# Decoder trunk on one core: modulation rows summed in 256 KB blocks from two buffers of their own, and four reorderings of issue

## The chip, the cores and the metric

The kernel runs on one core of a Trainium2 chip. Its time is the device time of one execution in microseconds; the median of several runs is what is compared. Engines are named as in the profile: PE (TensorE, the matrix engine) with PEld (its weight loads), DVE (VectorE), ACT (ScalarE), POOL (GpSimd) and SP (SyncE, which here does little else than issue DMAs). Each engine works through its own queue in order; a semaphore makes an instruction wait for another engine's or a DMA's result, and everything behind it on the same queue waits too.

## What is computed

One layer of a conditioned decoder trunk, sequence 512, width 1024, cut to its lines of substance:

```python
mod = silu(c) @ w_ada + b_ada                                   # (1024) @ (1024, 6*1024)
shift1, scale1, gate1, shift2, scale2, gate2 = split(mod, 6)
h = rmsnorm(x, norm1_g) * (1 + scale1) + shift1
qa, ka, va, qd, kd, vd, ga, gd = split(h @ w_in)                # input projection
out_a = sliding_window_attention(qa, ka, va, sinks)             # 8 heads, 2 kv heads, window 128
out_d = diff_attention(qd, kd, vd, lam, subln_g)                # 4 heads, softmax1 - lam * softmax2
merged = sigmoid(ga) * (out_a @ w_branch_swa) + sigmoid(gd) * (out_d @ w_branch_diff)
x = x + gate1 * (merged @ w_out)
h2 = rmsnorm(x, norm2_g) * (1 + scale2) + shift2
a, g = split(h2 @ w_up)                                         # 2 x 2816
a = causal_conv3(a) + conv_b
x = x + gate2 * ((gelu(a) * g) @ w_down)
return rmsnorm(x, final_g)
```

The modulation vector `mod` has six parts. The first two are needed at once; the other four (gate1, shift2, scale2, gate2, columns 2D to 6D of `w_ada`) are needed only behind the attention. Those four are the "modulation rows" here.

## The kernel before, in words

Everything stays in float32 accuracy: a float32 operand is split into a high part (cast on ACT) and a low part (subtraction on DVE), and each product takes three matmuls. So each weight tile of 512 KB passes through a raw buffer, gets an ACT cast `..._h` (L115) and a DVE subtraction `..._l` (L116), and then feeds PE. There are four raw buffers (`raw_tile`, tag "raw").

The kernel goes through these stages: the first modulation parts and the first norm (up to about 60 us); the attention with the input projection in between (to about 300 us); the branch gates and the merge; the output projection (`oc`, `wo`), the second norm and its transposes (`th`, about 345 to 375 us); the up products (`up`, from about 372 us on) and the down products (`dc`).

In the attention stage PE's order is written out by hand (`manual_schedule` for the tensor engine): scores, transposes and values of a window pair or of a differential block stand at fixed places, and between them `fill(n)` issues n steps of whatever projection is next (`units`: q, k and v of the differential heads, gates, branch products). Each step counts one tick. ACT's and DVE's order in this stage is not written by hand: a planner places their instructions, by priority and by when it holds their inputs for ready. SP's DMA order follows from the same planning. `tc.high_priority(offset=...)` lifts an instruction's priority. Behind the output projection the order of DVE, ACT, PE and POOL is written out by hand as well.

In the names of the trace: `sw`, `st`, `mx`, `nm`, `lsum` belong to the softmax of the window heads (four pairs; `tp` are its transposes on PE, `oa` and `outal` its values), `sd`, `dmx`, `dls` to the softmax of the differential heads (four heads of four blocks; `td` are its transposes on PE). `qkv` are the evictions of a head's projections.

The modulation rows are no matmul: `ada_rows` is a generator that `fill` advances every `ADA_EVERY` ticks. Each step loads two 128-row blocks of one half part (`ra`, 128x2x512, 512 KB, from SP), and adds both on DVE into `arow`, weighted by the column `cs` of silu(c): the first of eight blocks by a multiplication (L776), the other seven by multiply and add (L778). There are 4 parts x 2 halves x 8 blocks = 64 sums. When a half is done, `ada_spread` adds over the partitions by four small matmuls (`pr`), copies `row` on ACT (L794) and writes it to DRAM from POOL, from where it is later read as broadcast rows (`g1b`, `g2b`) or columns. Behind tick 20 a sum has a raised priority.

Further on the change touches: `add_head` (evictions of q and k), `diff_values` (`of`, and `rstd_m2`, a root that is worked out by DVE, POOL and DVE), the loads of the up weights of block 1 (`wa1_0`, `wa1_1`, cast by ACT and DVE as `early`, L1287 and L1291), and the modulation of the transposed rows (`mod_one`: `braw`<-`th`, L1255 on ACT, L1253 on DVE).

Of the kernel before, what the change touches and what calls it, by code (L numbers as in the profile page):

```python
# [8 lines left out]
F32 = mybir.dt.float32  # L9
# [5 lines left out]
P = 128  # L15
# [12 lines left out]
HP = 100000  # L28
ST = 6
ADA_LAG = 1  # L30
ADA_EVERY = 8
ADA_EASY = 20
ADA_START = 4
V_LAG = 13
# [19 lines left out]
def kernel(  # L54
# [130 lines left out]
    def rstd_m2(dst, ssq, n, d, wpool, plus=None):  # L185
        rstd_end(dst, *rstd_start(ssq, n, d, wpool, plus), n, wpool)
# [239 lines left out]
    def evac(hi, lo, src, scale=None):  # L426
        if scale is None:
            nc.scalar.copy(hi, src)
            nc.vector.tensor_sub(lo, src, hi.bitcast(F32))
        else:  # L430
            nc.scalar.activation(hi, src, AF.Copy, scale=scale)
            nc.vector.scalar_tensor_tensor(lo, src, scale, hi.bitcast(F32), ALU.mult, ALU.subtract)
# [184 lines left out]
    def add_head(h):  # L617
        def q(wts):
            t = heads[h] = ap.tile([P, 6, S], F32R, tag="qkv", bufs=2, name=f"qkv{h}")
            o = fbank(f"pq{h}")  # L620
            yield from steps(o, wts, hT, KT)
            evac(t[:, 0], t[:, 1], o, 2.0 ** (2 * h - 1))

        def k(wts):
            t = heads[h]
            o = fbank(f"pk{h}")
            yield from steps(o, wts, hT, KT)
            evac(t[:, 2], t[:, 3], o)

        def v(wts):  # L630
            t = heads[h]
            o = fbank(f"pw{h}")
            yield from steps(o, wts, hT, KT)
            vT = ap.tile([P, S], F32, tag="tmp", bufs=2, name=f"vT{h}")
            with tc.high_priority(offset=HP):
                nc.scalar.copy(vT, o)

            def turn():
                pv = tbank(f"pv{h}")
                for m in range(NT):  # L640
                    nc.tensor.transpose(pv[:, m * P : (m + 1) * P], vT[:, m * P : (m + 1) * P], ident)
                evac(t[:, 4], t[:, 5], pv)

            after(V_LAG, turn)

        for run, col in ((q, COL_QD), (k, COL_KD), (v, COL_VD)):
            units.append((lambda col=col: load_cols(win, col + h * P, f"w{col}_{h}"), run))
# [73 lines left out]
    def diff_values(h):  # L721
        t, (aTh, aTl) = heads[h], aTs[h]
        o = vbank(f"od{h}")
        for k in range(NT):
            q0 = k * P
            mm3(
                o[:, q0:], t[:, 4, k * P : (k + 1) * P], t[:, 5, k * P : (k + 1) * P],
                aTh[:, k * AW + q0 : k * AW + 512], aTl[:, k * AW + q0 : k * AW + 512],
                k == 0, k == NT - 1,
            )  # L730
        sq = ap.tile([P, S], F32, tag="tmp", bufs=2, name=f"sq{h}")
        of = ap.tile([P, S], F32, tag="of", bufs=2, name=f"of{h}")
        nc.scalar.activation(sq, o, AF.Square)
        nc.scalar.activation(of, o, AF.Copy, scale=sublnc)

        def stats():
            pss = tbank(f"pss{h}", (P, NT))
            for n in range(NT):
                nc.tensor.matmul(pss[:, n : n + 1], sq[:, n * P : (n + 1) * P], ones[:, 0:1], start=True, stop=True)
            rs = ap.tile([P, NT], F32, tag="drs", bufs=2, name=f"drs{h}")  # L740
            rstd_m2(rs, pss, NT, P, ap)

            def spread():
                rb = tbank(f"rb{h}")
                for n in range(NT):
                    nc.tensor.transpose(rb[:, n * P : (n + 1) * P], rs[:, n : n + 1].to_broadcast([P, P]), ident)
                nc.vector.tensor_mul(of, of, rb)
                split(outd[0][:, h], outd[1][:, h], of)

            after(NORM_LAG, spread)  # L750

        after(STAT_LAG, stats)


    mod_rows = tc.dram_tile([4, D], F32, name="mod_rows")

    def ada_load(idx, hf, k):
        c0 = (2 + idx) * D + hf * S
        r = raw_tile([P, 2, S], f"ra{idx}{hf}_{k}")
        nc.sync.dma_start(r, wada[k * P : (k + 2) * P, c0 : c0 + S].rearrange("(a p) n -> p a n", p=P))  # L760
        return r


    def ada_rows():
        todo = [(idx, hf, k) for idx in range(4) for hf in range(2) for k in range(0, KT, 2)]
        r = ada_load(*todo[0])
        yield
        for (idx, hf, k), job in zip(todo, todo[1:] + [None]):
            nxt = ada_load(*job) if job else None
            if k == 0:  # L770
                ac = big.tile([P, S], F32, tag=("sq2", "g2b1")[hf], name=f"arow{idx}{hf}")
            with tc.high_priority(offset=HP // 2) if tick[0] > ADA_EASY else ExitStack():
                for a in range(2):
                    cc = cs[:, k + a : k + a + 1]
                    if k + a == 0:
                        nc.vector.tensor_scalar_mul(ac, r[:, a], cc)  # L776
                    else:
                        nc.vector.scalar_tensor_tensor(ac, r[:, a], cc, ac, ALU.mult, ALU.add)  # L778
            if k == KT - 2:
                after(ADA_LAG, lambda idx=idx, hf=hf, ac=ac: ada_spread(idx, hf, ac))  # L780
            r = nxt
            yield


    def ada_spread(idx, hf, ac):
        pr = tbank(f"pr{idx}{hf}", (P, P))
        for g in range(4):
            gs = slice(32 * g, 32 * g + 32)
            nc.tensor.matmul(
                pr[gs], ones[:, gs], ac[:, g * P : (g + 1) * P], start=True, stop=True, tile_position=(0, 32 * g)  # L790
            )
        row = big.tile([P, P], F32, tag="g2b0", name=f"row{idx}{hf}")
        with tc.high_priority(offset=HP):
            nc.scalar.copy(row, pr)  # L794
        nc.gpsimd.dma_start(  # L795
            mod_rows[idx, hf * S : (hf + 1) * S].rearrange("(g n) -> g n", g=4), row[0:P:32]
        )
# [88 lines left out]
        add_gate_a(j)  # L886
    fill(4)
    diff_values(DIFF_HEADS - 1)
    while units or loaded or current:
        fill(1)  # L890
    at.close()


    bp = pool("mlp")

    def gpart(i, shape, name, dt=F32):
        return bp.tile(shape, dt, tag=f"gT{i}", name=name)
# [122 lines left out]
    bl = big.tile([P, 3, 4, 256], F32R, tag="hlA", name="bl")  # L1020
    braw = {}
    oacc = eight("oc")
    wo = [load_rows(wout, k, f"wo{k}", g1b) for k in range(KT)]

    def add_and_stat(acc, dst, x, wpool, name):
# [27 lines left out]
    early_w = [  # L1053
        big.tile([P, 2, 4, 256], F32R, tag=g, name=f"early{i}") for i, g in enumerate(("kvA", "kvB", "outh", "outl"))
    ]
    W, R = {}, {}

    def load_raw(dst, blocks):
        nc.sync.dma_start(dst, upblock(*blocks[0]))
# [44 lines left out]

    load_a(0, 0)
    load_a(0, 1)
    load_a(1, 0)
    load_a(1, 1)
    st = gpart(3, [P, 2, 4, 256], "s1_t1")
    t1n = st[:, 1]  # L1110
    R[0, "s1"] = load_raw(st[:, 0], [(0, 1, 0), (0, 1, 1)])
# [257 lines left out]
    mul_slot(0, "p2", (0,))  # L1369
    for g in (0, 1):  # L1370
        for kk in range(2):
            mod_one(b12[:, ks(g)], tps[g], g, kk)
        if g == 0:
            cast_w(0, "m5")
    for g in (2, 3):
        tps[g] = turn2(2, g)
    mul_slot(0, "p2", (1,))
    mul_slot(1, "p1", (1,))
    mul_slot(1, "p2")
    bV += [tbank("up6"), tbank("up7")]  # L1380
    V.tensor_sub(t1n[:, q0], b11[:, q0], b12[:, q0])
    low_w(0, "m5")
    V.tensor_sub(t1n[:, q1], b11[:, q1], b12[:, q1])
    sum_w(0, "m6")
    hi_t(0, t1n, q0)
    for kk in range(2):
# [429 lines left out]
```

## Time and profile before

| | |
|---|---|
| median of 3 runs | 702.29 us (701.95 to 703.43) |
| the profiled execution | 705.5 us, of which the span from first to last instruction is 703.6 us |
| mean granted TensorE clock | 0.992 |
| PE busy | 683.6 us, 97% of the span |
| DVE busy | 572.0 us, 81% |
| ACT busy | 375.8 us, 53% |
| POOL busy | 82.5 us, 12% |
| moved by DMA | 121.81 MB, mean 173 GB/s |

Times in the views are microseconds from the start of the span. A row of a timeline gives start, duration, engine, line, operation, output<-input, shape, how many in a row it stands for, and in brackets how long the engine stood idle just before it and what ended that. A row of waits gives the waiting instruction, what released it, the total, the number of times and the longest. A row of DMA issues gives the queue, how many, KB each and the median from issue to landing.

### The profile page before, as it was taken

What the parts mean: (1) busy time and instruction counts of PE and PEld (TensorE: products, weight loads), DVE (VectorE), ACT (ScalarE), POOL (GpSimd) and SP (SyncE); (2) the same over time, 40 slices, a digit from 0 to 9 for tenths busy, and PEclk for the clock granted to TensorE, in tenths of its full rate; (3) what the DMA queues carried; (4) which work ended last, traced back from release to release, by engine and by line L of the source; (5) the groups of instructions that cost most, each with busy time, mean ns of one, the idle gap of its engine ahead of it and who ended that gap; (6) DMA issues with size and microseconds to landing.
All of it is one profiled execution on the core that took longest, in us unless ns stands there. A gap on an engine that the chain in (4) does not pass through costs nothing. (4 is left out here: it accounts for less than half of the span.)

```text
span 703.6 us, 11256 instructions
## 1 busy us (share of the span) xinstructions
PE 683.6 (97%) x4203; PEld 595.5 (85%) x4203; DVE 572.0 (81%) x1098; ACT 375.8 (53%) x668; POOL 82.5 (12%) x100
## 2 busy tenths in 40 slices
PE   5999999999999999999999999999999999999995
PEld 5777776777788888888889999999999999888884
DVE  4999887887886567663579999888889899979996
ACT  4545766455543333331368656555656666655664
POOL 3000000001000100000021111111111102540300
PEclk8999999999999999999999999999999999999998
DMA  9885455354435676229617798886879738996903
GB/s 312 276 266 175 142 155 154 91 159 130 134 118 148 190 238 201 92 92 280 197 32 150 182 203 201 194 207 183 205 204 222 171 126 227 185 202 198 165 1 119
DMA packets 115862, 121.81 MB, mean 173 GB/s; under 512 B 4383, under 2 KB 93280, under 8 KB 115808
## 3 DMA queue, kind: packets, MB, share of 16 engines
q1 hardware_dynamic: 96894, 95.09, 42.8%
q0 software_dynamic: 18720, 25.73, 21.9%
q8 instruction: 33, 0.54, 0.3%
q10 hardware_dynamic: 194, 0.28, 0.1%
q14 instruction: 21, 0.17, 0.1%
HBM read 118.97 MB, written 2.11 MB: 172 GB/s over the span
## 5 line engine op out<-in xcount | busy, mean ns | idle before, releaser
L1150 PE MATMUL up<-t,m_whi 128*128 128x256 f32 x528 | 96.1, 283 | 0.0
L1150 PEld LDWEIGHTS up<-t,m_whi 128*128 128x128 f32 x528 | 82.4, 192 | 0.0
L1150 PE MATMUL up<-t,m_wlo 128*128 128x256 f32 x264 | 74.6, 283 | 0.2 <-DVE m_wlo L1093 0.2
L1150 PE MATMUL up<-bl,p_whi 128*128 128x256 f32 x232 | 65.6, 283 | 0.0
L1150 PE MATMUL up<-bh,p_whi 128*128 128x256 f32 x232 | 65.6, 283 | 0.0
L1150 PE MATMUL up<-bh,p_wlo 128*128 128x256 f32 x232 | 65.5, 283 | 0.0
L778 DVE SCALAR_TENSOR_TENSOR arow<-ra,cs,arow 128x512 f32<-128x512 f32 x56 | 41.9, 748 | 23.3 <-DMA ra<-in_w_ada_dram 22.9
L1150 PEld LDWEIGHTS up<-t,m_wlo 128*128 128x128 f32 x264 | 50.6, 192 | 0.4 <-DVE m_wlo L1093 0.4
L1150 PEld LDWEIGHTS up<-bh,p_whi 128*128 128x128 f32 x232 | 44.5, 192 | 0.0
L1150 PEld LDWEIGHTS up<-bl,p_whi 128*128 128x128 f32 x232 | 44.5, 192 | 0.0
L1150 PEld LDWEIGHTS up<-bh,p_wlo 128*128 128x128 f32 x232 | 44.5, 192 | 0.0
L1061 POOL DMA_DIRECT2D s<-in_w_up_dram x21 | 27.0, 1360 | 142.4 <-DMA s<-in_w_up_dram 77.5
L1093 DVE TENSOR_TENSOR m_wlo<-s,m_whi 128x1024 fp32r<-128x1024 f32 x31 | 37.8, 1218 | 0.9 <-ACT m_whi L1089 0.9
L1089 ACT CAST m_whi<-s 128x1024 fp32r<-128x1024 f32 x31 | 32.4, 1047 | 9.6 <-DVE s L1083 6.4
L1150 PE MATMUL up<-t,p_whi 128*128 128x256 f32 x176 | 32.3, 284 | 0.3 <-DVE pairs L1190 0.3
L173 POOL TENSOR_TENSOR r<-ms,mhalf 128x1 f32<-128x1 f32 (+1 forms) x16 | 12.8, 803 | 135.7 <-DVE ms L171 75.4
L795 POOL DMA_DIRECT2D mod_rows<-row x8 | 5.1, 642 | 197.5 <-ACT row L794 197.5
L1150 PEld LDWEIGHTS up<-t,p_whi 128*128 128x128 f32 x176 | 27.4, 192 | 0.5 <-issue 0.4
L698 ACT ACTIVATE sd<-sd,dmx 128x128 f32<-128x128 f32 (+3 forms) x32 | 17.7, 556 | 18.7 <-DVE dmx L690 18.7
L1157 ACT ACTIVATE gT<-a,cv 128x512 f32<-128x512 f32 x22 | 17.7, 813 | 17.6 <-DVE a L1192 17.3
L1089 ACT CAST p_whi<-wa 128x1024 fp32r<-128x1024 f32 x18 | 18.7, 1040 | 12.0 <-PE up L1150 10.8
L1150 PE MATMUL up<-t,p_wlo 128*128 128x256 f32 x88 | 24.9, 283 | 0.0
(474 smaller groups left out, 2055.6 us busy)
## 6 DMA issues: line engine op xcount, KB each, us to landing
ra<-in_w_ada_dram SPq DMA_DIRECT2D x32, 512.0 KB, 4.0
wa<-in_w_up_dram SPq DMA_DIRECT2D x22, 512.0 KB, 4.6
s<-in_w_up_dram SPq DMA_DIRECT2D x21, 512.0 KB, 5.2
s<-in_w_up_dram POOLq DMA_DIRECT2D x21, 512.0 KB, 7.7
adaw<-in_w_ada_dram SPq DMA_DIRECT2D x16, 512.0 KB, 4.8
w<-in_w_in_dram SPq DMA_DIRECT2D x12, 512.0 KB, 4.0
a<-in_w_up_dram SPq DMA_DIRECT2D x11, 512.0 KB, 4.8
b<-in_w_down_dram SPq DMA_DIRECT2D x10, 512.0 KB, 3.9
```

The source lines that it names most:

```text
L173: nc.gpsimd.tensor_tensor(r0, ms, mhalf[:, :n], ALU.pow)
L698: exp = nc.scalar.activation(pm[m], pm[m], AF.Exp, bias=mx[:, m : m + 1], scale=slope, accum_out=lsum[:, m : m + 1])
L778: nc.vector.scalar_tensor_tensor(ac, r[:, a], cc, ac, ALU.mult, ALU.add)
L795: nc.gpsimd.dma_start(mod_rows[idx, hf * S : (hf + 1) * S].rearrange("(g n) -> g n", g=4), row[0:P:32])
L1061: nc.gpsimd.dma_start(dst, upblock(*blk), accum_op=ALU.add)
L1089: nc.scalar.copy(W[J, name][0], R[J, SRC[name]])
L1093: nc.vector.tensor_sub(lo, R[J, SRC[name]], hi.bitcast(F32))
L1150: nc.tensor.matmul(o[u], w[:, k, cu], b[:, k], start=name in ("p1", "m5", "p2") and k == 0 and x == 0, stop=k == 3 and x == 2, skip_group_ ...
L1157: nc.scalar.activation(grow(j), av[J][:, u], AF.Identity, bias=cv[:, 66 + j : 67 + j], scale=cv[:, 44 + j : 45 + j])
```

## The change

In words: the 32 loads of two blocks become 64 loads of one block (256 KB). They leave the raw ring; even blocks have a buffer under the tag `g2b0`, odd blocks one in the attention's pool (tag `ra`) and, once that pool is closed, one under `gT0`. The load of block n+2 is issued one call of the generator after sum n, and the generator is advanced every second tick, so a sum comes every fourth. `row` gets a tile of its own. The reorderings: q's and k's evictions at high priority; the end of the statistics' root four ticks later (`ROOT_LAG`), with one buffer for `of`; the two loads of block 1's up weights early and into a buffer of their own (`wa1`) instead of through the raw ring behind the output weights; two of the four modulations of one turn on DVE instead of ACT, with a cast and a pair of subtractions moved accordingly.

```diff
@@ -28,7 +28,8 @@
 HP = 100000
 ST = 6
 ADA_LAG = 1
-ADA_EVERY = 8
+ROOT_LAG = 4
+ADA_EVERY = 2
 ADA_EASY = 20
 ADA_START = 4
 V_LAG = 13
@@ -619,13 +620,15 @@
             t = heads[h] = ap.tile([P, 6, S], F32R, tag="qkv", bufs=2, name=f"qkv{h}")
             o = fbank(f"pq{h}")
             yield from steps(o, wts, hT, KT)
-            evac(t[:, 0], t[:, 1], o, 2.0 ** (2 * h - 1))
+            with tc.high_priority(offset=HP):
+                evac(t[:, 0], t[:, 1], o, 2.0 ** (2 * h - 1))
 
         def k(wts):
             t = heads[h]
             o = fbank(f"pk{h}")
             yield from steps(o, wts, hT, KT)
-            evac(t[:, 2], t[:, 3], o)
+            with tc.high_priority(offset=HP):
+                evac(t[:, 2], t[:, 3], o)
 
         def v(wts):
             t = heads[h]
@@ -729,7 +732,7 @@
                 k == 0, k == NT - 1,
             )
         sq = ap.tile([P, S], F32, tag="tmp", bufs=2, name=f"sq{h}")
-        of = ap.tile([P, S], F32, tag="of", bufs=2, name=f"of{h}")
+        of = ap.tile([P, S], F32, tag="of", name=f"of{h}")
         nc.scalar.activation(sq, o, AF.Square)
         nc.scalar.activation(of, o, AF.Copy, scale=sublnc)
 
@@ -738,7 +741,8 @@
             for n in range(NT):
                 nc.tensor.matmul(pss[:, n : n + 1], sq[:, n * P : (n + 1) * P], ones[:, 0:1], start=True, stop=True)
             rs = ap.tile([P, NT], F32, tag="drs", bufs=2, name=f"drs{h}")
-            rstd_m2(rs, pss, NT, P, ap)
+            root = rstd_start(pss, NT, P, ap)
+            after(ROOT_LAG, lambda: rstd_end(rs, *root, NT, ap))
 
             def spread():
                 rb = tbank(f"rb{h}")
@@ -754,31 +758,44 @@
 
     mod_rows = tc.dram_tile([4, D], F32, name="mod_rows")
 
-    def ada_load(idx, hf, k):
+
+    ada_pool, ada_held = [ap], [False]
+
+    def ada_load(n, idx, hf, k):
         c0 = (2 + idx) * D + hf * S
-        r = raw_tile([P, 2, S], f"ra{idx}{hf}_{k}")
-        nc.sync.dma_start(r, wada[k * P : (k + 2) * P, c0 : c0 + S].rearrange("(a p) n -> p a n", p=P))
+        if n % 2 == 0:
+            r = big.tile([P, S], F32, tag="g2b0", name=f"ra{n}")
+        else:
+            home, tag = (ap, "ra") if ada_pool[0] is ap else (bp, "gT0")
+            r = home.tile([P, S], F32, tag=tag, name=f"ra{n}")
+        nc.sync.dma_start(r, wada[k * P : (k + 1) * P, c0 : c0 + S])
         return r
 
 
     def ada_rows():
-        todo = [(idx, hf, k) for idx in range(4) for hf in range(2) for k in range(0, KT, 2)]
-        r = ada_load(*todo[0])
-        yield
-        for (idx, hf, k), job in zip(todo, todo[1:] + [None]):
-            nxt = ada_load(*job) if job else None
+        todo = [(idx, hf, k) for idx in range(4) for hf in range(2) for k in range(KT)]
+        blocks = []
+        for n in range(2):
+            blocks.append(ada_load(n, *todo[n]))
+            yield
+        for n, (idx, hf, k) in enumerate(todo):
+            r = blocks.pop(0)
+            cc = cs[:, k : k + 1]
             if k == 0:
                 ac = big.tile([P, S], F32, tag=("sq2", "g2b1")[hf], name=f"arow{idx}{hf}")
             with tc.high_priority(offset=HP // 2) if tick[0] > ADA_EASY else ExitStack():
-                for a in range(2):
-                    cc = cs[:, k + a : k + a + 1]
-                    if k + a == 0:
-                        nc.vector.tensor_scalar_mul(ac, r[:, a], cc)
-                    else:
-                        nc.vector.scalar_tensor_tensor(ac, r[:, a], cc, ac, ALU.mult, ALU.add)
-            if k == KT - 2:
+                if k == 0:
+                    nc.vector.tensor_scalar_mul(ac, r, cc)
+                else:
+                    nc.vector.scalar_tensor_tensor(ac, r, cc, ac, ALU.mult, ALU.add)
+            if k == KT - 1:
                 after(ADA_LAG, lambda idx=idx, hf=hf, ac=ac: ada_spread(idx, hf, ac))
-            r = nxt
+            yield
+            if n + 2 < len(todo):
+                while ada_pool[0] is None and n % 2:
+                    ada_held[0] = True
+                    yield
+                blocks.append(ada_load(n + 2, *todo[n + 2]))
             yield
 
 
@@ -789,7 +806,7 @@
             nc.tensor.matmul(
                 pr[gs], ones[:, gs], ac[:, g * P : (g + 1) * P], start=True, stop=True, tile_position=(0, 32 * g)
             )
-        row = big.tile([P, P], F32, tag="g2b0", name=f"row{idx}{hf}")
+        row = cpool.tile([P, P], F32, tag="row", name=f"row{idx}{hf}")
         with tc.high_priority(offset=HP):
             nc.scalar.copy(row, pr)
         nc.gpsimd.dma_start(
@@ -886,12 +903,16 @@
         add_gate_a(j)
     fill(4)
     diff_values(DIFF_HEADS - 1)
-    while units or loaded or current:
+    while units:
+        fill(1)
+    ada_pool[0] = None
+    while loaded or current or not ada_held[0]:
         fill(1)
     at.close()
 
 
     bp = pool("mlp")
+    ada_pool[0] = bp
 
     def gpart(i, shape, name, dt=F32):
         return bp.tile(shape, dt, tag=f"gT{i}", name=name)
@@ -1020,6 +1041,10 @@
     bl = big.tile([P, 3, 4, 256], F32R, tag="hlA", name="bl")
     braw = {}
     oacc = eight("oc")
+    wa1 = gpart(2, [P, 2, 4, 256], "wa1")
+    for h in range(2):
+        c1 = 2 * P
+        nc.sync.dma_start(wa1[:, h], wup.rearrange("(h a p) n -> p h a n", h=2, a=4)[:, h, :, c1 : c1 + 2 * P])
     wo = [load_rows(wout, k, f"wo{k}", g1b) for k in range(KT)]
 
     def add_and_stat(acc, dst, x, wpool, name):
@@ -1053,7 +1078,7 @@
     early_w = [
         big.tile([P, 2, 4, 256], F32R, tag=g, name=f"early{i}") for i, g in enumerate(("kvA", "kvB", "outh", "outl"))
     ]
-    W, R = {}, {}
+    W, R = {}, {(1, f"a1{h + 1}"): wa1[:, h] for h in range(2)}
 
     def load_raw(dst, blocks):
         nc.sync.dma_start(dst, upblock(*blocks[0]))
@@ -1104,8 +1129,6 @@
 
     load_a(0, 0)
     load_a(0, 1)
-    load_a(1, 0)
-    load_a(1, 1)
     st = gpart(3, [P, 2, 4, 256], "s1_t1")
     t1n = st[:, 1]
     R[0, "s1"] = load_raw(st[:, 0], [(0, 1, 0), (0, 1, 1)])
@@ -1369,18 +1392,17 @@
     mul_slot(0, "p2", (0,))
     for g in (0, 1):
         for kk in range(2):
-            mod_one(b12[:, ks(g)], tps[g], g, kk)
-        if g == 0:
-            cast_w(0, "m5")
+            mod_one(b12[:, ks(g)], tps[g], g, kk, kk == 1)
+    cast_w(0, "m5")
     for g in (2, 3):
         tps[g] = turn2(2, g)
     mul_slot(0, "p2", (1,))
     mul_slot(1, "p1", (1,))
     mul_slot(1, "p2")
     bV += [tbank("up6"), tbank("up7")]
-    V.tensor_sub(t1n[:, q0], b11[:, q0], b12[:, q0])
+    for q in (q0, q1):
+        V.tensor_sub(t1n[:, q], b11[:, q], b12[:, q])
     low_w(0, "m5")
-    V.tensor_sub(t1n[:, q1], b11[:, q1], b12[:, q1])
     sum_w(0, "m6")
     hi_t(0, t1n, q0)
     for kk in range(2):
```

## The prediction

> **What bounds the kernel now.** I read the engine totals of the page first, then the table by stage, then the waits of TensorE (PE), and only then the rows of the tile that the change is about.
>
> ```profile
> PE 683.6 (97%) x4203; PEld 595.5 (85%) x4203; DVE 572.0 (81%) x1098; ACT 375.8 (53%) x668; POOL 82.5 (12%) x100
> ...
> core 0: us, PE busy (x) PEld busy (x) DVE busy (x) ACT busy (x) POOL busy (x), PEclk, DMA share, GB/s
> 60.00:100.00 40.00, 39.46 (x265) 30.68 (x264) 34.11 (x113) 26.42 (x78) 0.00 (x0) 1.00 0.52 157
> 100.00:130.00 30.00, 29.36 (x186) 22.14 (x182) 23.28 (x73) 16.81 (x46) 0.77 (x1) 1.00 0.46 141
> ...
> 150.00:220.00 70.00, 70.00 (x394) 56.29 (x393) 55.80 (x151) 34.99 (x80) 4.84 (x5) 1.00 0.47 136
> 220.00:345.00 125.00, 125.00 (x580) 101.49 (x579) 75.22 (x94) 37.82 (x50) 7.40 (x11) 1.00 0.60 182
> 345.00:375.00 30.00, 28.13 (x169) 24.55 (x168) 21.32 (x45) 19.24 (x39) 6.93 (x7) 1.00 0.37 81
> 375.00:400.00 25.00, 24.74 (x207) 24.57 (x206) 24.89 (x32) 18.10 (x29) 1.28 (x1) 1.00 0.67 158
> ```
>
> PE is busy 97% of the span, and no edit takes a matmul away. So the time can move only by PE's idle stretches. The table shows how few there are in the part that the change touches: nothing from 150 to 345 us, about half a us in each of the attention stages around 100 us, and 1.87 us between 345 and 375. The waits name them.
>
> ```profile
> PE th L1245 <- DVE xn L1235: 1.2, 1, 1.2
> PE th L1245 <- ACT braw L1255: 0.7, 1, 0.7
> PE tp L595 <- ACT row L794: 0.6, 1, 0.6
> PE sw L126 <- DVE outal L429: 0.4, 1, 0.4
> PE up L1150 <- DVE pairs L1190: 0.3, 1, 0.3
> PE td L716 <- DVE dls L701: 0.2, 1, 0.2
> PE up L1150 <- DVE m_wlo L1093: 0.2, 1, 0.2
> PE sw L126 <- DVE mx L561: 0.2, 1, 0.2
> ```
>
> Together these are 3.8 us. That is the ceiling of any gain: 1.4 us in attention (tp, sw twice, td), 1.9 us at the turns behind the output projection (th twice), 0.5 us in the first up products. A loss has no such ceiling, and the rows of the modulation sums show where one could come from.
>
> ```profile
> L778 DVE SCALAR_TENSOR_TENSOR arow<-ra,cs,arow x56: 736/750/755, 63.1 to 273.6; 128x512 f32<-128x512 f32 x56
> ...
>   DMA ra<-in_w_ada_dram: 27.0, 17
> ...
> ra<-in_w_ada_dram SPq DMA_DIRECT2D x32, 512.0 KB, 4.0
> ...
> out_dram<-x SPq DMA_DIRECT2D x2, 512.0 KB, 2.9
> ...
> out_dram<-x SPq DMA_DIRECT2D x3, 256.0 KB, 2.0
> ```
>
> DVE already stands 27.0 us, 17 times, waiting for these weights, and PE feels almost none of it. DVE works through its queue in order, so what counts is not how long it waits but which softmax step stands behind the wait.
>
> **Part 1, the sums in single blocks.** The 64 sums stay (56 at 750 ns), with the same bytes. What changes is the supply. Before, 32 loads of 512 KB pass through the four raw buffers that the projection weights use too, and each load feeds two sums. After, 64 loads of 256 KB pass through two buffers of their own, and load n+2 cannot be issued until sum n has been done. A buffer is therefore used once per round trip: the sum, SP's issue, the landing. A fresh 512 KB load can be timed from its issue to the sum that waited for it, together with the station where that happens:
>
> ```profile
> 119.98 11.34 SPq L760 DMA_DIRECT2D ra<-in_w_ada_dram  x3
> ...
> 120.78 0.28 DVE L680 CUSTOM_DVE_ANT_0 sd<-sd,ddf 128x128 f32<-128x128 f32 x1
> ...
> 123.65 0.75 DVE L778 SCALAR_TENSOR_TENSOR arow<-ra,cs,arow 128x512 f32<-128x512 f32 x1 [1.48 <-DMA ra<-in_w_ada_dram]
> ...
> 125.62 0.35 DVE L704 SCALAR_TENSOR_TENSOR sd<-sd,dls,sd 128x128 f32<-128x128 f32 x1
> ...
> 127.06 0.27 PE L716 MATMUL td<-ident,sd 128*128 128x128 f32 x1
> ```
>
> That is 123.65 - 119.98 = 3.67 us. Half the bytes saved 0.9 us on the output rows (2.9 against 2.0), so I take 2.8 us for a quiet 256 KB load and 0.7 + 2.8 = 3.5 us for the round trip, or 1.75 us per sum from two buffers. Bounds: 2.7 us if it landed like the 256 KB output rows (2.0), 4.7 us if halving saved nothing (4.0). I take 3.6, because a few of these loads (ra18, ra22, ra23) leave SP right beside a 512 KB projection weight.
>
> The Trainium skill ("SBUF — State Buffer", section "The DMA setup-cost knee") says that a transfer pays a roughly fixed 2 us besides its bytes at 436 GB/s and that transfers should be made as large as one can, which speaks against splitting. By its fit 512 KB would be an estimated 3.2 us, under the trace's 3.67, and 256 KB an estimated 2.6 us; the round trip would be 3.3 instead of 3.5, and the sum below about 1.8 us lower than with my 3.6, which is no change at all.
>
> Now the order of issue. The planner orders DVE, and a sum has high priority: wherever it holds the weights for landed, the sum goes first. Counting in the changed order, 8 sums stand ahead of the maximum of window pair 2 (12 before), but 24 stand ahead of the first differential maximum, sd at 120.78 (20 before). So the early part is lighter and the part from pair 2 on has to pass 16 sums where it passed 8.
>
> ```profile
> 89.85 0.29 DVE L561 CUSTOM_DVE_ANT_0 st<-sw,dsw 128x128 f32<-128x128 f32 x1
> ...
> 84.92 2.00 PE L126 MATMUL sw<-ka,qa 64*128 64x128 f32 x24
> ...
> 92.34 0.36 DVE L572 TENSOR_SCALAR nm<-mx,nsink 128x4 f32<-128x4 f32 x2
> ...
> 106.05 0.35 DVE L572 TENSOR_SCALAR nm<-mx,nsink 128x4 f32<-128x4 f32 x2
> ...
> 111.75 0.68 DVE L429 TENSOR_TENSOR outal<-oa,outah 128x512 fp32r<-128x512 f32 x1
> ```
>
> The lighter part: PE has pair 2's scores by 86.9, but DVE gets to them at 89.85. With fewer sums in front I walk DVE to the end of nm at about 90.6 instead of 92.6, and pair 3's nm ends about 1 us sooner than now (106.3). The stalls of sw (0.2 and 0.4) go with that, and tp's 0.6 goes because row's copy now stands between the exponentials of pair 3 and no longer behind a cast: 1.2 us.
>
> The heavier part: from pair 3's nm at 105.2 the sums ra14 to ra23 are ten, and the even ones form a chain 14, 16, 18, 20, 22, one round trip each. At 3.5 us: ra16 at 108.7, ra18 at 112.2 (just ahead of outal, now 111.75), ra20 and ra22 at about 116.5 and 120.0, partly held by DVE's own work between (two qkv evictions of outal's size and two casts of 128x1024, 1.2 each like early's further down), ra23 at 122.2, then outal and the first differential maximum at 123.5 against 120.78. From that maximum to the first finished block sd takes 125.62 + 0.35 - 120.78 = 5.2 us now, of which the waiting and two sums go (1.48 out of the exponentials' shadow, 0.75 once more); I take 4.4, so 127.9. PE wants it at 127.06 less the 1.2 just gained, 125.9. So PE stands about 2 us where it did not stand, and is 0.9 us behind the old time.
>
> The next two lumps are of the same kind. These rows give the old margins.
>
> ```profile
> 138.71 0.48 DVE L776 TENSOR_SCALAR arow<-ra,cs 128x512 f32<-128x512 f32 x1
> ...
> 145.78 0.35 DVE L704 SCALAR_TENSOR_TENSOR sd<-sd,dls,sd 128x128 f32<-128x128 f32 x1
> ...
> 146.28 0.30 PE L716 MATMUL td<-ident,sd 128*128 128x128 f32 x1 [0.20 <-DVE dls L701]
> ...
> 168.57 0.35 DVE L704 SCALAR_TENSOR_TENSOR sd<-sd,dls,sd 128x128 f32<-128x128 f32 x1
> ...
> 170.37 0.27 PE L716 MATMUL td<-ident,sd 128*128 128x128 f32 x1
> ```
>
> Head 1: ra24 starts some 3 us earlier than the 138.71 of now (the two sums inside head 0's softmax are gone), but ra24 to ra30 then all stand ahead of the last step of sd1's first block, where only two sums stand now. The chain 24, 26, 28, 30 is three round trips, 10.5 us, from 135.7: ra30 at 146.2, the block ready at 147.2 against 146.1 (145.78 + 0.35). Loss 1.1 us. Head 2: ra32 to ra37 stand ahead of the step that ends at 168.9; ra36 and ra37 are in front of it and bring it to about 170.9 against PE's 170.37. Loss 0.6 us. In head 3 and behind, the rows of 220 to 345 show DVE busy 75.22 of 125 us, and I find no step that becomes late.
>
> Attention at 3.5 us: 0.9 + 1.1 + 0.6 = +2.6. About six round trips in series bind, so each 0.1 us of the trip moves it 0.6; at 3.6 it is +3.2. At 2.7 the chains vanish and it is -1.4, the stalls of now and no more. At 4.7 it is +9.8.
>
> The other price of 64 loads is 32 more issues on SP, 368 ns each by the row below, 12 us in some 210. SP does nothing else with a deadline there, and projection weights gain, since the raw buffers are free of ra; I cost it at nothing. If SP became late, the weights' casts would be, and PE with them.
>
> ```profile
> L760 SPq DMA_DIRECT2D ra<-in_w_ada_dram x32: 367/368/374, 56.4 to 267.7; - x32
> ```
>
> The reused tag of the odd buffer lets the bias DMA on POOL wait for the last sum (about 274 us); DVE then waits for that landing, in a stage where it is 60% busy and PE never idle. Nothing.
>
> **Part 2, the reorderings.** Early evictions of q and k, one buffer for of, and the later end of the statistics' root: PE has not one idle us from 150 to 220 for these to win back, and they add no work. Nothing, between -0.2 and +0.3 (that margin of td at 146). The early load of block 1's up weights is worth something:
>
> ```profile
> 348.72 1.05 ACT L1287 CAST early<-wa 128x1024 fp32r<-128x1024 f32 x1 [1.92 <-DMA wa<-in_w_up_dram]
> ...
> 349.81 1.23 DVE L1291 TENSOR_TENSOR early<-wa,early 128x1024 fp32r<-128x1024 f32 x1 [1.75 <-ACT early L1287]
> 350.95 1.28 DVE L1216 TENSOR_TENSOR x<-x,oc 128x512 f32<-128x512 f32 x2
> ```
>
> Now the cast waits for its weights, DVE's low half waits for the cast, and the first residual add stands behind it. With the weights there by then, the add starts about 1.1 us sooner and the norms behind it too, so of the 1.2 us at th about 1.1 go. The 0.7 at the second th goes because DVE takes two of the four modulations from ACT (braw), and that bank comes free sooner. But from 375 to 400 DVE is busy 24.89 of 25 us: it has to carry its work, with two modulations more (128x256, so less than outal's 0.68 each; about 1.0 together), through to its end either way. DVE gains the 1.1 us and the waits inside it, some 1.4 by the two th rows, and gives 1.0 back: I take -1.5 us for PE, with the small stalls at up (0.5) remaining. Bounds -0.5 (DVE gives nearly all of it back) and -2.4 (all of th and up).
>
> **Sum.** +3.2 - 1.5 = +1.7 us: 705.5 + 1.7 = 707.2 in a profiled execution, and since the runs without profile stood 3.2 us below the profiled one, 702.3 + 1.7 = 704.0 us. What a measurement of this kernel tells from no change is about 0.2%, 1.4 us.
>
> **The rivals.** (A) The forecast: round trip 3.3 to 3.9, attention +1.4 to +5.0, net 0 to +3.5, so 702.2 to 705.8. For it: the chain can be read off the order. Against it: 27.0 us of such waits cost PE next to nothing so far. (B) The other side: the waits stay under cover, because a landing is nearer to the output rows' 2.0 or DVE has more slack than I walk; attention -1.4 to 0, with part 2 net -1.5 to -3.5: 698.8 to 700.8, at 700 most likely. It decides at a round trip of 3.1 us or less. (C) Landing is not shortened by halving, as the 4.0 us median of loads in company hints: round trip 4.2 to 4.7, attention +6.8 to +9.8, net +5 to +8: 707.5 to 710.5, first of all at the td of 127 and 146. (D) Gains and losses cancel within 1.4 us; that is the low end of A.
>
> **Chances.** A 0.50 (of it slower by over 1.4 us 0.35, within 0.15), B 0.31 (faster), C 0.15, something else that holds DVE or SP up 0.04 (half slower, half faster). Faster 0.33, the same 0.15, slower 0.52. The range reaches from the middle of B to the beginning of C, 699.3 to 708.5; A alone is 702.2 to 705.8.
>
> **What would show it.** In the profile of the changed kernel: the landing of ra, whose median I expect at 2.8 to 3.2; the row "DMA ra" under the tile's idle time, which I expect above 27 us, at 35 to 50, in more and shorter waits; PE waiting at td for DVE's sd near 127, 146 and 170, 2, 1 and 0.6 us; no wait of tp for row, of sw for outal, or of the first th for xn. It is wrong if PE shows no new wait at td (then B), or if the new waits stand at 220 to 345, where I see none.

## The result, and the profile after

The changed kernel takes 721.24 us (median of 6 runs, 717.5 to 722.84) against 702.12 us before: 19.1 us slower by the medians. The ratio of the runs is 1.0252 (95% interval 1.0232 to 1.0273), which would be 17.7 us; what versions cost or take back is reckoned below from the medians, where nothing else is said. The profiled execution spans 720.7 us against 703.6, at a mean granted clock of 0.985 against 0.992. The forecast was 704.0 with a range up to 708.5: the direction was right, the size was not.

First the engine totals and then what PE waited for, as before. PE's busy time grew by 4 us although it does the same matmuls, and the list of its waits is another one.

```profile
PE 687.8 (95%) x4203; PEld 598.1 (83%) x4203; DVE 574.0 (80%) x1100; ACT 375.3 (52%) x666; POOL 82.2 (11%) x100
```

```profile
PE td L719 <- DVE dls L704: 5.7, 2, 3.1
PE tp L596 <- DVE qkv L430: 4.9, 1, 4.9
...
PE sw L127 <- DVE outal L430: 2.0, 2, 1.2
PE pss L742 <- DVE qkv L430: 1.7, 1, 1.7
...
PE up L1173 <- DVE pairs L1213: 0.5, 1, 0.5
PE up L1173 <- DVE m_wlo L1118: 0.5, 2, 0.3
```

The waits of th are gone, as forecast. In attention there are 14.3 us of waits (td, tp, sw, pss) where there were 1.4. All of them end with a DVE instruction. The tile of the sums shows what DVE itself stood for: 29.0 us in 26 waits where it was 27.0 in 17. Hardly more in total, but in other places.

```profile
L771 SPq DMA_DIRECT2D ra<-in_w_ada_dram x64: 327/328/1768, 46.4 to 291.5; - x64
...
  DMA ra<-in_w_ada_dram: 29.0, 26
  PE pr L806: 0.4, 1
...
DMA to landing us min/median/max: 2.6/3.4/5.5
```

The longest wait of PE shows how it happens. These are DVE's rows of the changed kernel around window pair 3, then PE's.

```profile
107.00 1.52 DVE L790 SCALAR_TENSOR_TENSOR arow<-ra,cs,arow 128x512 f32<-128x512 f32 x2
110.62 0.49 DVE L788 TENSOR_SCALAR arow<-ra,cs 128x512 f32<-128x512 f32 x1 [2.10 <-DMA ra<-in_w_ada_dram]
...
113.83 0.75 DVE L790 SCALAR_TENSOR_TENSOR arow<-ra,cs,arow 128x512 f32<-128x512 f32 x1 [0.40 <-DMA ra<-in_w_ada_dram]
...
114.69 0.68 DVE L430 TENSOR_TENSOR outal<-oa,outah 128x512 fp32r<-128x512 f32 x1
...
116.08 0.68 DVE L430 TENSOR_TENSOR qkv<-pk,qkv 128x512 fp32r<-128x512 f32 x1
116.81 0.75 DVE L790 SCALAR_TENSOR_TENSOR arow<-ra,cs,arow 128x512 f32<-128x512 f32 x1
117.47 0.68 DVE L430 TENSOR_TENSOR qkv<-pv,qkv 128x512 fp32r<-128x512 f32 x1
```

```profile
118.21 0.90 PE L596 MATMUL tp<-ident,st 128*128 128x128 f32 x3 [4.94 <-DVE qkv L430]
...
155.50 0.30 PE L719 MATMUL td<-ident,sd 128*128 128x128 f32 x1 [3.14 <-DVE dls L704]
```

ra16 may be loaded only when ra14 has been added (107.00 to 107.7) and is added at 110.62: a round trip of 3.6 us, and DVE stands 2.10 us of it. Behind that sum wait the normalisation of pair 3, `outal`, the eviction of `pk`, three more sums (one of which waits 0.40 us again) and last the eviction of `pv`. That one is no softmax step at all, but `pv` lies in one of the two PSUM banks (tag "t") that PE's transposes `tp` use. PE stands 4.94 us until the eviction ends at 118.15. From the start of pv's own transposes on PE to the end of that eviction it is 14.2 us here and 9.7 us in the kernel before (103.96 to 113.69).

The second part of the loss is in the clock column of the table by stage (columns: stretch, its length, busy time of PE, PEld, DVE, ACT, POOL, then PEclk, DMA share, GB/s).

```profile
112.00:118.00 6.00, 1.20 (x6) 0.49 (x5) 5.52 (x16) 2.28 (x4) 0.00 (x0) 0.78 0.49 135
118.00:121.00 3.00, 2.79 (x8) 2.36 (x9) 2.57 (x4) 0.48 (x1) 0.00 (x0) 0.50 0.53 163
121.00:124.00 3.00, 3.00 (x15) 2.30 (x13) 0.89 (x2) 1.00 (x3) 0.00 (x0) 0.80 0.78 247
...
224.00:230.00 6.00, 6.00 (x23) 4.78 (x23) 4.06 (x13) 2.28 (x5) 1.25 (x1) 0.72 0.06 21
```

PE comes back from the 4.94 us wait at half the clock (0.50 from 118 to 121). It is busy there, so no wait tells of it. The same stands behind the 1.67 us wait at pss (0.72 from 224 to 230), which is again for an eviction of `pv`, DVE's row first:

```profile
222.27 0.69 DVE L430 TENSOR_TENSOR qkv<-pv,qkv 128x512 fp32r<-128x512 f32 x1
```

```profile
223.10 1.02 PE L742 MATMUL pss<-ones,sq 128*128 128x1 f32 x8 [1.67 <-DVE qkv L430]
```

How much the clock costs can be read from PE's fixed order, by the same two instructions, the kernel before first:

```profile
62.81 0.95 PE L126 MATMUL sw<-ka,qa 64*128 64x128 f32 x12
...
195.26 0.27 PE L716 MATMUL td<-ident,sd 128*128 128x128 f32 x1
```

```profile
61.66 0.96 PE L127 MATMUL sw<-ka,qa 64*128 64x128 f32 x12
...
210.06 0.27 PE L719 MATMUL td<-ident,sd 128*128 128x128 f32 x1
```

The first `sw` row starts 1.2 us earlier than before (61.66 against 62.81), the first `td` of head 3 at 210.06 against 195.26, 14.8 us later. So 16.0 us were lost between; the waits of sw, tp and td explain 12.6, less the 1.4 of before, 11.2. The other 4.8 us are work at a lowered clock. The table by stage over just this stretch bears it out (before, then changed): the same 799 matmuls keep PE busy 4.6 us longer, at a mean clock of 0.95.

```profile
62.81:195.26 132.45, 131.07 (x799) 101.97 (x799) 110.46 (x340) 73.74 (x203) 5.33 (x6) 1.00 0.47 140
```

```profile
61.66:210.06 148.40, 135.63 (x799) 106.01 (x799) 113.60 (x344) 73.93 (x203) 4.65 (x6) 0.95 0.44 132
```

The runs of the changed kernel spread with it: the two with a mean clock of 0.989 and 0.990 took 718.67 and 717.5 us, the four with 0.985 took 720.5 to 722.8.

### The profile page after: what moved, and what is told of

Its sections match the earlier page's. It is cut to its first block, busy times and chain, and to the rows that moved or that the text cites. A ratio compares the mean times of both kernels' runs of the same rounds, so it can differ in the third digit from the quotient of the medians.

```text
span 720.7 us, 11320 instructions
## 1 busy us (share of the span) xinstructions
PE 687.8 (95%) x4203; PEld 598.1 (83%) x4203; DVE 574.0 (80%) x1100; ACT 375.3 (52%) x666; POOL 82.2 (11%) x100
## 5 line engine op out<-in xcount | busy, mean ns | idle before, releaser
L174 POOL TENSOR_TENSOR r<-ms,mhalf 128x1 f32<-128x1 f32 (+1 forms) x16 | 12.6, 786 | 154.9 <-DVE ms L172 74.4
L701 ACT ACTIVATE sd<-sd,dmx 128x128 f32<-128x128 f32 (+3 forms) x32 | 17.7, 556 | 18.4 <-DVE dmx L693 17.5
L1180 ACT ACTIVATE gT<-a,cv 128x512 f32<-128x512 f32 x22 | 17.7, 813 | 17.7 <-DVE a L1215 17.3
L1114 ACT CAST p_whi<-wa 128x1024 fp32r<-128x1024 f32 x18 | 18.7, 1041 | 11.8 <-PE up L1173 10.5
L1118 DVE TENSOR_TENSOR p_wlo<-wa,p_whi 128x1024 fp32r<-128x1024 f32 x18 | 22.0, 1221 | 3.5 <-ACT p_whi L1114 2.9
```

The source lines that it names most:

```text
L174: nc.gpsimd.tensor_tensor(r0, ms, mhalf[:, :n], ALU.pow)
L701: exp = nc.scalar.activation(pm[m], pm[m], AF.Exp, bias=mx[:, m : m + 1], scale=slope, accum_out=lsum[:, m : m + 1])
L1114: nc.scalar.copy(W[J, name][0], R[J, SRC[name]])
L1118: nc.vector.tensor_sub(lo, R[J, SRC[name]], hi.bitcast(F32))
L1180: nc.scalar.activation(grow(j), av[J][:, u], AF.Identity, bias=cv[:, 66 + j : 67 + j], scale=cv[:, 44 + j : 45 + j])
```

## The experiments

Fifteen kernels, in four groups on one chip each, with the kernel before beside them. T1 is the theory of the forecast: two buffers make DVE wait a round trip, in places where softmax steps stand behind. T2: the raised evictions of q and k push the eviction of `pv` back, and that holds PE's bank. T3: the sums' own time and rank ahead of the softmax steps is the loss, loads or not. The planner orders DVE anew in every version, and the banks seem to be given out with it, so no version changes one thing alone.

**Parts alone.** The reorderings without the single blocks (`ADA_EVERY` 8, loads and buffers as before):

> The kernel before with the four reorderings alone, the sums as they were (32 loads of 512 KB through the raw ring). Theory T1 (the two-buffer round trip of the sums is the loss): no wait of 2 us or more in attention, and the waits at th are gone, so 701.0 us (700 to 702). Theory T2 (the early q and k evictions push the eviction of pv back, and that holds a PSUM bank which PE's transposes need): the loss shows without the single blocks too, PE waits for DVE qkv near 113 and 221 us, 707 us or more.

Measured 702.13 us, ratio 1.0003 (0.9994 to 1.0012): no loss, but no gain either, and just outside the 700 to 702 us of T1. So the reorderings do not lose by themselves; T2 alone is refuted. The waits at th are gone, but waits of 0.7 at td and twice 0.5 at tp stand in attention.

The single blocks without the reorderings (`of` single, for space):

> The change's single blocks in two own buffers with a sum every fourth tick, and of the reorderings only the single buffer of the tile of (the space needs it). T1: nearly the whole loss, 721 to 724 us, PE waits at td as in the changed kernel. T2: the 4.9 us wait at tp and the 1.7 us wait at pss go, with the clock that they cost, so 712 to 715 us.

Measured 716.69 us, 1.0208 (1.0186 to 1.0230), 14.6 us slower than before. The blocks carry three quarters of the loss, the reorderings add some 4.5 us on top of them. Both theories missed: T1 too high, T2 too low. The wait at tp for `qkv` is still 4.5 us, so the raised evictions do not make it; what goes without the reorderings is the wait at pss and most of that at sw (2.0 to 0.5 us).

The q and k evictions at ordinary priority, the rest as changed:

```diff
-            with tc.high_priority(offset=HP):
-                evac(t[:, 0], t[:, 1], o, 2.0 ** (2 * h - 1))
+            evac(t[:, 0], t[:, 1], o, 2.0 ** (2 * h - 1))
...
-            with tc.high_priority(offset=HP):
-                evac(t[:, 2], t[:, 3], o)
+            evac(t[:, 2], t[:, 3], o)
```

> The changed kernel without the raised priority of the q and k evictions. T1: within 2 us of the changed kernel, 719 to 723 us. T2: the waits for DVE qkv at tp (4.9 us) and pss (1.7 us) go and some 3 us of lowered clock behind them, so 711 to 714 us; the waits at td (5.7 us) stay.

Measured 715.73 us, 1.0194 (1.0174 to 1.0214), between the two: below T1's 719 to 723, above T2's 711 to 714. In DVE's queue `pv` now goes ahead of `pk`, but behind the same sums, so PE's wait at tp falls from 4.9 only to 4.1 us:

```profile
107.63 0.49 DVE L786 TENSOR_SCALAR arow<-ra,cs 128x512 f32<-128x512 f32 x1 [1.51 <-DMA ra<-in_w_ada_dram]
...
113.75 0.68 DVE L430 TENSOR_TENSOR qkv<-pv,qkv 128x512 fp32r<-128x512 f32 x1
...
115.20 0.68 DVE L430 TENSOR_TENSOR qkv<-pk,qkv 128x512 fp32r<-128x512 f32 x1
```

**A third buffer.** The running sum keeps one tile, the other becomes a buffer:

```diff
-        if n % 2 == 0:
-            r = big.tile([P, S], F32, tag="g2b0", name=f"ra{n}")
+        if n % 3 != 1:
+            r = big.tile([P, S], F32, tag=f"g2b{n % 3 // 2}", name=f"ra{n}")
...
-                ac = big.tile([P, S], F32, tag=("sq2", "g2b1")[hf], name=f"arow{idx}{hf}")
+                ac = big.tile([P, S], F32, tag="sq2", name=f"arow{idx}{hf}")
...
-            if n + 2 < len(todo):
+            if n + 3 < len(todo):
```

> The changed kernel with three own buffers instead of two, loads three blocks ahead; the running sum then has one tile instead of two, so that the first sum of a half waits for the reduction of the half before. T1: half again the supply, the DMA wait of DVE for ra falls from 29 us to 12 or less, the td waits fall under 2 us in total, 707 to 712 us. T2: the waits for DVE qkv stay, 716 us or more.

Measured 706.0 us, 1.0054 (1.0037 to 1.0071). One buffer more takes back 15 of the 19 us, although it adds waits for the reduction `pr`; that is 1 us better than T1's range. Of the experiments this one speaks most for T1: the waits for `qkv`, which T2 had staying, are gone, and DVE's wait for ra falls to 8.0 us. Its rows: first what PE waits for in attention, then DVE in front of the sums, then DVE around pair 3.

```profile
PE td L719 <- DVE dls L704: 1.8, 1, 1.8
...
PE sw L127 <- DVE mx L562: 0.8, 1, 0.8
...
PE tp L596 <- ACT pT L598: 0.7, 1, 0.7
```

```profile
  DMA ra<-in_w_ada_dram: 8.0, 7
  PE pr L806: 2.7, 3
```

```profile
107.86 0.66 DVE L430 TENSOR_TENSOR outal<-oa,outah 128x512 fp32r<-128x512 f32 x1
...
109.42 0.69 DVE L430 TENSOR_TENSOR qkv<-pk,qkv 128x512 fp32r<-128x512 f32 x1
110.02 0.75 DVE L790 SCALAR_TENSOR_TENSOR arow<-ra,cs,arow 128x512 f32<-128x512 f32 x1
110.68 0.69 DVE L430 TENSOR_TENSOR qkv<-pv,qkv 128x512 fp32r<-128x512 f32 x1
```

The order from `outal` to `pv` is that of the changed kernel, but no sum waits there, and from pv's transposes to the end of its eviction it is 9.2 us, about what it was before. That is not all that saves PE: its second tile of transposes waits 0.7 us for ACT's copy `pT` of the first and no longer for `pv`, so it reads as if the planner had given it the other bank. The 1.8 us wait at td is the one of head 1. There eight sums stand ahead of the step that PE needs (seven in the changed kernel) and none of them waits for its load, so that wait comes from the sums' place.

**No loads.** Every sum reads the one block that is loaded (`blocks.append(r)` in place of the load):

> The changed kernel with one block loaded once and all 64 sums taken from it, so 63 of the 64 loads are left out and the modulation rows are other values; sums, ticks and priorities stay. T1: DVE never waits for ra in attention, no wait of PE of 1.5 us or more there, 700 to 702 us. A rival T3, that the sums' own DVE time and their rank ahead of the softmax steps is the loss: the td waits stay at 1 us or more each, 707 us or more.

Measured 708.98 us, 1.0096 (1.0069 to 1.0123). T1 missed here: without any wait for a load DVE is still late at td, with the sums, now always ready, standing ahead of the softmax steps.

```profile
PE td L719 <- DVE dls L704: 3.6, 2, 1.9
...
PE pa L266 <- DVE ac L259: 1.7, 1, 1.7
```

The pa wait lies before attention (53.7 us), where sums crowd in front of the first modulation. So T3 has a share: some 3.6 us of waits at td without any load. The wait at tp for `qkv` is gone, but that does not show that it needs the loads' waits: the transposes start at 114.51 us, behind ACT's `pT` again, before pv's eviction ends (115.28), so they do not use its bank here. What the loads' waits cost shows in that eviction itself: 10.5 us from pv's transposes to its end, against 14.2 in the changed kernel.

**The sums' rank.**

```diff
-            with tc.high_priority(offset=HP // 2) if tick[0] > ADA_EASY else ExitStack():
+            with ExitStack():
```

> The changed kernel with the sums at ordinary priority. T1: the waits of DVE for ra may stay, but stand behind softmax steps more often, so part of the loss goes: 708 to 716 us. T3: nearly all goes, 701 to 704 us. If the order by the planner's own reckoning of the landing is what puts them there, whatever their priority, nothing goes: 719 to 723 us.

Measured 713.34 us, 1.0149 (1.0131 to 1.0167), 8 us of the 19 back, as T1 had it: td falls from 5.7 to 3.5 us, tp from 4.9 to 4.1.

**The eviction of pv raised** like those of q and k:

> The changed kernel with the eviction of pv, whose bank PE's next transposes need, raised like those of q and k. T2 as far as it is left: the 4.9 us wait at tp shrinks to 2 us or less and the 1.7 us at pss goes, 714 to 717 us. T1 alone: DVE stands in front of a sum before the eviction anyway, wait at tp 3 us or more, 718 us or more.

Measured 712.29 us, 1.0134 (1.0116 to 1.0151), 9 us back, more than T2 had expected. The wait at tp shrinks and that at pss goes, those at td stay:

```profile
PE td L720 <- DVE dls L705: 6.2, 3, 3.0
...
PE tp L596 <- DVE st L585: 1.8, 2, 1.3
...
PE sw L127 <- DVE outal L430: 1.2, 1, 1.2
```

The waits in attention are 9.2 us here against 14.3, so they explain 5 of the 9 us. The rest fits the clock, which in the profiled execution stays at 1.00 behind the td waits (last section).

The parts overlap: 15 (third buffer), 9 (pv) and 8 us (rank) are more than 19 together. The long stall at tp needs a sum that waits, an eviction behind it, and transposes that were given that eviction's bank.

**Halving alone.** The kernel before with single blocks in the shared ring of four, one load ahead:

> The kernel before with its sums' loads cut to single blocks of 256 KB, but in the shared ring of four and one load ahead, a sum every fourth tick; no reordering. If halving the transfers is what costs (64 landings instead of 32), 710 us or more and DVE waits for ra over 40 us. T1 (a buffer comes round only after its own sum and a landing): here one load is under way beside each sum as with two buffers, so the chain is nearly as bad: 706 to 716 us, DVE waiting 30 us or more. If only the privacy of the two buffers costs: 702 us.

Measured 708.86 us, 1.0076 (1.0056 to 1.0096), in T1's range: DVE waits 38.1 us in 31 pieces, and the same two stalls stand there as in the changed kernel (tp for qkv 3.2, pss for qkv 1.1), though nothing else was changed. The waits at td do not stand there.

**The middle of the kernel.** The early load of block 1 and the modulations on DVE alone:

> The kernel before with the early load of block 1's up weights and the two modulations on DVE alone. T1, as forecast for this part: the waits at th (1.2 and 0.7 us) go, some comes back at up, 700.2 us against 701.7 (by -1.5, between -2.4 and -0.5). A rival: DVE gives it all back, no change.

Measured 702.38 us against 702.85, ratio 0.9988 (0.9979 to 0.9998): a gain of 0.8 us, inside the bounds and half the value taken. It is the one version whose interval lies below 1, and only just; the next one, with the same edit in it, does not repeat it.

> The kernel before with the early load of block 1's up weights, the two modulations on DVE and a tile of its own for row. Expected from the rows of mid_only: its 0.7 us wait of tp for row goes if the copy moves ahead; then 701.5 against 702.4. If the copy's place in ACT's order does not come from the tile, no further change, 702.3.

Measured 702.7 us, 0.9996 (0.9984 to 1.0008). The own tile alone does not remove the wait: tp still waits 0.6 us for row. In the changed kernel that wait is gone; which other part moved the copy is not shown.

**Can the blocks be saved?** Three buffers with the sums at ordinary rank, and the same with `pv` raised:

> Three own buffers and the sums at ordinary priority. T1 and T3 together: with supply enough, what is left of the loss (1.8 us at td and the clock behind it) is the sums' rank ahead of the softmax steps, so 701 to 704 us. If the rank matters only while DVE waits for loads, 705 to 707 us as with three buffers alone.

> Three own buffers, sums at ordinary priority and pv's eviction raised like q's and k's. As three_low, with no wait for qkv or pT at tp: 700 to 703 us. If pv's eviction ahead of softmax steps makes those late, td waits of 1 us or more come back: 704 us or more.

Measured 703.98 us, 1.0020 (1.0008 to 1.0032), and 704.2 us, 1.0022 (1.0007 to 1.0037). The first lies in its range of 701 to 704 us, the second just above its 700 to 703, where a td wait was to come back. Rank and supply together leave 1.5 us, one td wait (2.3 and 1.8 us) among it. Neither beats the kernel before.

**What one stall costs.** A chain of small DVE operations in front of one transpose, at the end of gate 6:

```diff
+            if j == 6:
+                scr = cpool.tile([P, P], F32, tag="scr", name="scr")
+                with tc.high_priority(offset=HP):
+                    nc.vector.tensor_scalar_mul(scr, o[:, :P], 1.0)
+                    for _ in range(2):
+                        nc.vector.tensor_scalar_mul(scr, scr, 1.0)
+                pscr = tbank("pscr", (P, P))
+                nc.tensor.transpose(pscr, scr, ident)
...
```

The two longer ones have `range(6)` and `range(13)`.

> The kernel before with one artificial stall of PE at the end of gate 6, near 245 us, where PE has no other idle time: three dependent DVE operations of 128x128, one transpose of the result, one copy. Reckoned stall 0.9 to 1.3 us. If a stall costs its own length, 702.8 us plus 1.1 = 703.9; if any stall also lowers the granted clock behind it, 705 us or more.

> As stall_short with seven DVE operations: a stall of about 1.8 to 2.3 us. Its own length alone: 704.8 us. With a lowered clock behind it as behind the 1.67 us wait of the changed kernel: 706 to 707 us, and a granted clock near 0.5 for some us in the table by stage.

> As stall_short with fourteen DVE operations: a stall of about 3.4 to 4.2 us. Its own length alone: 706.6 us. With a lowered clock: 708 to 709 us.

The lengths missed their aim, since the chain's first operation had to wait in DVE's order: PE stood 6.8, 7.0 and 12.0 us. The kernels took 711.45, 712.03 and 717.28 us, ratios 1.0131 (1.0110 to 1.0153), 1.0143 (1.0113 to 1.0172) and 1.0213 (1.0196 to 1.0231), so by the ratios 9.2, 10.0 and 15.0 us more than the kernel before: each time the profiled stall and 2.4 to 3.0 us besides, whatever its length. By PE's fixed order 1.7, 2.6 and 1.7 us of that lie between the `rb` transposes in front of the stall and the first `pm` matmul behind it, against the kernel before; the rest lies elsewhere and was not traced. The table by stage of stall_long shows about 1.5 us of it: 2.5 us of work at 0.50, then 3 us at 0.92.

```profile
239.00:251.00 12.00, 0.44 (x2) 0.00 (x1) 9.85 (x22) 2.80 (x4) 1.03 (x2) 0.72 0.43 142
251.00:254.00 3.00, 2.51 (x7) 2.06 (x8) 1.61 (x4) 0.27 (x1) 0.00 (x0) 0.50 0.77 193
254.00:257.00 3.00, 3.00 (x14) 2.44 (x13) 0.69 (x1) 0.00 (x0) 0.00 (x0) 0.92 0.43 157
```

Stalls of 1 to 4 us, which were meant, stay untried by this means.

## Why the prediction was right in direction and wrong in size

- **The bound, and where time can come from: right as to the place, not as to "only by PE's idle stretches".** The loss is in attention, but PE's clock carries part of it beside the idle time.
- **The round trip: right where it was walked, short over the whole.** 3.6 us was taken and 3.6 us stands in the rows of ra14 and ra16. From 100 to 160 us the median landing is 2.8 us, within the 2.8 to 3.2 named; from 160 to 220 us it is 3.8, and 3.4 over all 64. By the Trainium skill ("SBUF — State Buffer", section "The DMA setup-cost knee") 256 KB would take an estimated 2.6 us, which is the minimum of the tile's row, no more.
- **"From pair 3's nm ... the sums ra14 to ra23": the step that failed.** The walk followed softmax results to the transposes and nothing else. It left out that DVE also evicts `pv`, and that PE's next transpose needs that bank. At tp, where the walk had only a gain of 0.6 us, PE stood 4.94; where it found "no step that becomes late" behind head 3, PE stood 1.67 at pss for the same kind of eviction, in the 220 to 345 us that the prediction named as a sign of being wrong. That pv_high takes back 9 us, 5 of them in waits, shows how much lies in it.
- **Head 0: wrong the other way.** The forecast 2 us at the first td did not come; the stall at tp had come earlier and covered it. In pv_high, where tp waits 1.8 us in all, that td waits 0.53.
- **Head 1 and 2: right in place, too small.** 1.1 and 0.6 us were reckoned, 3.14 and 2.58 measured. The walk took DVE's own work as packed; in the trace a cast's low half waits 0.82 us for ACT and ra28 lands 1.26 us late, one behind the other. Part was the sums' place, as three_buffers shows (1.8 us at head 1 with no such wait).

```profile
144.52 1.22 DVE L117 TENSOR_TENSOR w_l<-w,w_h 128x1024 fp32r<-128x1024 f32 x1 [0.82 <-ACT w_h L116]
...
150.78 0.75 DVE L790 SCALAR_TENSOR_TENSOR arow<-ra,cs,arow 128x512 f32<-128x512 f32 x1 [1.26 <-DMA ra<-in_w_ada_dram]
```

```profile
184.01 0.45 PE L719 MATMUL td<-ident,sd 128*128 128x128 f32 x1 [2.58 <-DVE dls L704]
```

- **"The stalls of sw go": wrong.** They grew from 0.6 to 2.0 us, at 85 and 99 us; both times `outal` stands behind sums that waited for their loads.
- **DVE's wait for ra, "35 to 50 us": wrong.** 29.0 us. The sum of such waits said nothing of the loss, as the paragraph on the bound itself had it; three buffers with 8.0 us and the kernel before with 27.0 are 4 us apart in the other direction.
- **The clock: left out.** No term stood for it, and it cost 4.8 us up to head 3 and more behind. It is a term that the sum put at nothing without a reason.
- **Attention as a whole:** +3.2 us was the term, the PE order shows 16.0 us by head 3 already.
- **The reorderings: right alone, wrong in company.** For the middle -1.5 us was taken and -0.8 measured; all four together on the old loads are nothing (reorder_only). But the raised evictions of q and k, put at "nothing, between -0.2 and +0.3", cost some 5 us once the sums wait (715.73 without them against 721.24). The 32 more SP issues show no wait of their own; no run has them alone.
- **The rival that came was none of the three in size.** C had the mechanism of too long chains, at up to 710.5 us, but by slow landings. Where the largest stall stands the landings were as reckoned; it was what stood behind them. (C's +5 to +8 on 702.3 are 707.3 to 710.3, not 707.5 to 710.5, and the range up to 708.5 reaches 1 us into C.) That the direction came out right is partly luck: the largest wait was not in the sum at all, and the first term of the sum did not come.

## What to carry to other kernels

Behind an in-order engine's wait, go through everything queued there, and ask of each instruction not only who reads its result but whose bank or buffer it frees. A buffer that comes round only after use and landing gives one block per round trip; here a third buffer took back more (15 us) than either change of priority (8 and 9). And a stall of the matrix engine is to be priced at its length and, where it lowers the clock, some 2 us more (1.7 to 2.6 us in the three made stalls).

## What the runs showed of the hardware that was not expected

The granted clock does not follow the length of a wait alone. In the changed kernel it fell behind waits of 4.94, 3.14, 2.58 and 1.67 us (0.50 from 118 to 121, 0.66 from 155 to 160, 0.62 from 184 to 188, 0.72 from 224 to 230). In pv_high a wait of 3.0 us at the same td as the 3.14 one left it at 1.00, in the one execution of each that was profiled:

```profile
146.00:149.00 3.00, 0.82 (x4) 0.36 (x2) 3.00 (x8) 0.00 (x0) 0.00 (x0) 1.00 0.43 126
149.00:153.00 4.00, 3.17 (x18) 2.90 (x19) 2.52 (x8) 1.23 (x3) 0.00 (x0) 1.00 0.84 266
```

The Trainium skill ("TensorE: Matmul & The Clock Gate", section "Part 1: The HAM clock gate") says that the clock halves after about 3.4 us of idle and comes back after about 3.4 us of work, counted in a window that runs on by itself. The halving (0.50), the length of the slow stretch (some 3 us at 0.50, then a mixed one) and the chance in it agree with these rows; the 3.4 us of idle do not, since 1.67 us were enough here. Over the profiled executions of all these kernels, from 60 to 300 us, each of the seven waits of 3.1 to 4.9 us was followed by work at 0.50. Of the fourteen waits from 1.5 to 3.0 us five were (the shortest 1.52, in three_low) and nine were not; of the six from 1.1 to 1.4 us, none. What decides it between 1.5 and 3 us, no run here shows.
